# Every other tile of a streaming GELU-and-multiply kernel in two steps, of seven rows and of one

## Chip, cores, metric

One Trainium2 chip, one core of it. The metric is the device time of one execution in microseconds (us). Differences are told as the ratio of the means of the runs of the same rounds, with a 95% interval; within 2% counts as the same.

## The reference

The input is 32 x 512 x 2048 floats (134 MB), the output 32 x 512 x 1024 (67 MB).

```python
def reference(x):
    half_dim = x.shape[-1] // 2
    x1, x2 = x[..., :half_dim], x[..., half_dim:]
    gelu_x1 = 0.5 * x1 * (1 + erf(x1 / np.sqrt(2)))
    return (gelu_x1 * x2).astype(np.float32)
```

## The kernel before

The 16384 rows are cut into 16 tiles of 128 partitions x 8 rows. A tile is loaded whole (8.39 MB) through the Scalar engine's DMA queue, GELU runs in place on the Scalar engine (ACT), the multiply on the Vector engine (DVE), and the result (4.19 MB) is stored through the Sync engine's queue. There are two input and two output buffers. Tiles 0 and 15 are done in steps of 2, 2 and 4 rows, so that the start and the end are short. A transfer is issued when an engine hands it to its queue, and has landed when whatever waits for it may go on; in the profile a q behind an engine's name marks that issuing side.

```python
x_tiles = [xpool.tile([P, R, dim], x.dtype, name=f"x{k}_tile") for k in range(2)]
o_tiles = [opool.tile([P, R, half], out.dtype, name=f"o{k}_tile") for k in range(2)]
...
load(0)
load(1)
for i in range(n_tiles):
    x_tile, o_tile = x_tiles[i % 2], o_tiles[i % 2]
    last = i == n_tiles - 1
    pieces = i == 0 or last
    steps = ((0, 2), (2, 4), (4, 8)) if pieces else ((0, 8),)
    for lo, hi in steps:
        rows = slice(lo, hi)
        gelu = ... nc.scalar.activation(out=x_tile[:, rows, :half], in_=x_tile[:, rows, :half], func=GELU)
        mul = nc.vector.tensor_mul(out=o_tile[:, rows, :], in0=x_tile[:, rows, :half], in1=x_tile[:, rows, half:])
        ...
        if pieces and hi % 4 == 0:
            part = slice(hi - 4, hi)
            nc.sync.dma_start(out=o_t[i][:, part, :], in_=o_tile[:, part, :])
    if not pieces:
        nc.sync.dma_start(out=o_t[i], in_=o_tile)
    ...
    if i + 2 < n_tiles:
        load(i + 2)        # into the buffer that tile i has just left
```

Of the kernel before, what the change touches and what calls it, by code (L numbers as in the profile page):

```python
# [1 line left out]

# [4 lines left out]

GELU = mybir.ActivationFunctionType.Gelu


@with_exitstack
def kernel(
    ctx: ExitStack,
    tc: tile.TileContext,
    x: bass.AP,
    out: bass.AP,
):











    nc = tc.nc
    P = nc.NUM_PARTITIONS  # L30

    x_flat = x.flatten_outer_dims()
    out_flat = out.flatten_outer_dims()
    n_rows, dim = x_flat.shape
    half = dim // 2

    R = 8
    x_t = x_flat.rearrange("(n p r) d -> n p r d", p=P, r=R)
    o_t = out_flat.rearrange("(n p r) d -> n p r d", p=P, r=R)
    n_tiles = x_t.shape[0]  # L40

    xpool = ctx.enter_context(tc.tile_pool(name="xpool", bufs=1))
    opool = ctx.enter_context(tc.tile_pool(name="opool", bufs=1))
    x_tiles = [xpool.tile([P, R, dim], x.dtype, name=f"x{k}_tile") for k in range(2)]
    o_tiles = [opool.tile([P, R, half], out.dtype, name=f"o{k}_tile") for k in range(2)]

    def no_wait(ins, others):
        for other in others:
            tc.declare_no_dep(ins, other, reason="implied by another wait")

    x_users, o_users = ([], []), ([], [])
    loads = {}

    def load(i):
        x_tile = x_tiles[i % 2]
        loads[i] = []
        for rows in (slice(0, 4), slice(4, 8)) if i == 0 else (slice(0, 8),):
            dma = nc.scalar.dma_start(out=x_tile[:, rows, :], in_=x_t[i][:, rows, :])  # L58
            loads[i].append(dma.ins)
# [4 lines that stand above are left out]
        x_tile, o_tile = x_tiles[i % 2], o_tiles[i % 2]  # L64
        last = i == n_tiles - 1
        pieces = i == 0 or last
        steps = ((0, 2), (2, 4), (4, 8)) if pieces else ((0, 8),)
        gelus, muls = [], []
        for lo, hi in steps:
            rows = slice(lo, hi)  # L70
            gelu = tc.keep_in_program_order(
                nc.scalar.activation(  # L72
                    out=x_tile[:, rows, :half], in_=x_tile[:, rows, :half], func=GELU
                )
            )
            no_wait(gelu.ins, x_users[i % 2])
            mul = nc.vector.tensor_mul(  # L77
                out=o_tile[:, rows, :],
                in0=x_tile[:, rows, :half],
                in1=x_tile[:, rows, half:],  # L80
            )
            no_wait(mul.ins, loads[i] + x_users[i % 2] + o_users[i % 2])
            gelus.append(gelu.ins)
            muls.append(mul.ins)
# [5 lines that stand above are left out]
        x_users[i % 2].extend(gelus + muls + loads[i])  # L90
        o_users[i % 2].extend(muls)
        if i + 2 < n_tiles:
            load(i + 2)


# [1 line left out]
_INS = ['x']  # L97
_OUTS = [((32, 512, 1024), 'float32')]


# [23 lines left out]
```

## Time and profile before

| | before |
|---|---|
| time, median of 3 runs | 470.62 us |
| span of the profiled run | 468.8 us |
| busy: DVE, ACT | 30%, 24% |
| moved, over the span | 201.33 MB at 429 GB/s |
| one tile period in the steady part | 29.0 us |
| a load, from issue to landing | 42.2 us (median) |

The lines of the profile are in the prediction.

### The profile page before, as it was taken

How to read it: one execution, taken by the hardware profiler on the slowest of the kernel's cores; microseconds unless marked ns; L12 is line 12 of the kernel's file. 1: busy time of each engine (PE TensorE's matmuls, PEld its weight loads, DVE VectorE, ACT ScalarE, POOL GpSimd, SP SyncE). 2: the span in 40 equal slices, each digit the busy share in tenths (PEclk: the TensorE clock that was granted, in tenths of full speed). 3: DMA queues.
4: the chain of work that ended last, by engine and by line, in shares of the span. 5: the costliest groups of instructions: out<-in, count | busy, mean ns of one | idle time of the engine just before them, and what ended most of it. 6: DMA issues, size and time to landing. Idle time of an engine off the chain costs nothing.

```text
span 468.8 us, 150 instructions
## 1 busy us (share of the span) xinstructions
DVE 139.5 (30%) x20; ACT 114.2 (24%) x21; POOL 0.2 (0%) x4
## 2 busy tenths in 40 slices
DVE  0330333407033070430704207052070510606142
ACT  1320505041050410505005050140501405023060
POOL 0000000000000000000000000000000000000000
DMA  8999999999999999999999999999999999999998
GB/s 358 447 447 447 414 389 495 403 403 447 481 414 403 447 403 492 403 433 417 492 403 403 447 492 403 403 447 447 447 403 439 411 492 403 403 447 492 403 403 358
DMA packets 5041, 201.33 MB, mean 429 GB/s; under 512 B 561, under 2 KB 561, under 8 KB 561
## 3 DMA queue, kind: packets, MB, share of 16 engines
q10 hardware_dynamic: 2448, 134.22, 66.3%
q1 hardware_dynamic: 2592, 67.11, 33.2%
q14 instruction: 1, 0.00, 0.0%
HBM read 134.22 MB, written 67.11 MB: 429 GB/s over the span
## 4 chain that ended last, share of the span: by engine, by line
DMA 72%; DVE 14%; ACT 12%; ACTq 1%; issue 0%
DMA x_tile<-in_x_dram 72%; DVE o_tile L77 14%; ACT x_tile L72 12%; ACTq L119 0%; ACTq L58 0%
## 5 line engine op out<-in xcount | busy, mean ns | idle before, releaser
L77 DVE TENSOR_TENSOR o_tile<-x_tile 128x8192 f32<-128x8192 f32 (+2 forms) x20 | 139.5, 6985 | 320.7 <-ACT x_tile L72 320.7
L72 ACT ACTIVATE x_tile<-x_tile 128x8192 f32<-128x8192 f32 (+2 forms) x20 | 113.0, 5662 | 339.4 <-DMA x_tile<-in_x_dram 339.4
L72 ACT ACT_TABLE_LOAD x1 | 1.3, 1283 | 2.1 <-issue 2.1
L108 POOL MEMSET const-bfloat16-1.0<- 128x1 bf16 x1 | 0.1, 102 | 0.0
L108 POOL MEMSET const-uint8-127<- 128x1 uint8 x1 | 0.1, 102 | 0.0
L108 POOL MEMSET const-float32-0.0<- 128x1 f32 x1 | 0.1, 99 | 0.2 <-issue 0.2
L108 POOL MEMSET const-float32-1.0<- 128x1 f32 x1 | 0.1, 99 | 0.0
## 6 DMA issues: line engine op xcount, KB each, us to landing
out_dram<-o_tile SPq DMA_DIRECT2D x14, 4096.0 KB, 42.4
x_tile<-in_x_dram ACTq DMA_DIRECT2D x2, 4096.0 KB, 16.8
out_dram<-o_tile SPq DMA_DIRECT2D x4, 2048.0 KB, 18.0
x_tile<-in_x_dram ACTq DMA_DIRECT2D x15, 42.2
```

The lines of the kernel that those rows point to most:

```text
L72: nc.scalar.activation(out=x_tile[:, rows, :half], in_=x_tile[:, rows, :half], func=GELU)
L77: mul = nc.vector.tensor_mul(out=o_tile[:, rows, :], in0=x_tile[:, rows, :half], in1=x_tile[:, rows, half:],)
L108: nc = _bacc.Bacc("TRN2", target_bir_lowering=False, num_devices=1)
```

## The change

The intent: let the multiply of an odd tile start once seven eighths of its GELU are done. Its end, and with it the next load into that buffer, then comes earlier by about one row's GELU, less what the added instructions cost.

```diff
-        steps = ((0, 2), (2, 4), (4, 8)) if pieces else ((0, 8),)
+        steps = ((0, 2), (2, 4), (4, 8)) if pieces else ((0, 7), (7, 8)) if i % 2 else ((0, 8),)
```

## The prediction

> **What bounds the kernel now.** I read the page first, for what is full. Engines, then the transfer lines of the slices, then the queues:
>
> ```profile
> span 468.8 us, 150 instructions
> DVE 139.5 (30%) x20; ACT 114.2 (24%) x21; POOL 0.2 (0%) x4
> DMA  8999999999999999999999999999999999999998
> q10 hardware_dynamic: 2448, 134.22, 66.3%
> q1 hardware_dynamic: 2592, 67.11, 33.2%
> DMA x_tile<-in_x_dram 72%; DVE o_tile L77 14%; ACT x_tile L72 12%; ACTq L119 0%; ACTq L58 0%
> ```
>
> The two compute engines are under a third busy. The 16 DMA engines are at "9" in every slice but the first and the last, and the two queues' packet times add up to 66.3 + 33.2 = 99.5% of 16 engines' span. That leaves next to no idle transfer time to win. The last line, however, puts 14 + 12 = 26% of the chain that ended last on the multiply and the GELU. The chain names whatever released the next step, not whatever was full, so I had to look at whether these 26% are really in series with the transfers.
>
> The busy view by stretches, one tile period (29 us) each, decides it. Columns: stretch and length, busy time of DVE, ACT, POOL with instruction counts, clock, DMA share, GB/s.
>
> ```profile
> 71.00:100.00 29.00, 8.69 (x1) 7.03 (x1) 0.00 (x0) 1.00 1.00 434
> 100.00:129.00 29.00, 8.69 (x1) 7.03 (x1) 0.00 (x0) 1.00 1.00 434
> 158.00:187.00 29.00, 8.69 (x1) 7.03 (x1) 0.00 (x0) 1.00 1.00 434
> ```
>
> Share 1.00 and 434 GB/s, period after period, while a GELU and a multiply run in each. No period has a hole while compute runs.
>
> Why compute makes no hole shows in the timeline (start, length, engine, instruction, idle before it):
>
> ```profile
> 158.41 7.03 ACT L72 ACTIVATE x_tile<-x_tile 128x8192 f32<-128x8192 f32 x1 [22.00 <-DMA x_tile<-in_x_dram]
> 165.47 8.69 DVE L77 TENSOR_TENSOR o_tile<-x_tile 128x8192 f32<-128x8192 f32 x1 [20.33 <-ACT x_tile L72]
> 174.20 0.37 ACTq L58 DMA_DIRECT2D x_tile<-in_x_dram  x1
> 187.40 7.03 ACT L72 ACTIVATE x_tile<-x_tile 128x8192 f32<-128x8192 f32 x1 [21.96 <-DMA x_tile<-in_x_dram]
> ```
>
> Tile 5 landed at 158.4; its buffer is free when its multiply ends at 174.2, and only then is the load of tile 7 issued into it. But tile 6 is still on its way until 187.4. The load of tile 7 therefore lies queued for 187.4 - 174.2 = 13.2 us and moves from 187.4 to 216.4, when its own GELU starts: 29.0 us. The chain of waits books all of 174.20 to 216.37 as transfer:
>
> ```profile
> 158.41 7.04 ACT x_tile L72
> 165.47 8.70 DVE o_tile L77
> 174.20 42.17 DMA x_tile<-in_x_dram
> 216.39 7.04 ACT x_tile L72
> ```
>
> 42.17 = 13.2 queued + 29.0 moving. So the path through compute has 13.2 us of slack per tile, and the 26% of the chain lie beside the other tile's transfer.
>
> **What the Trainium skill says.** "DMA: Bandwidth & Descriptors", section "Queues, rings and completion order": each DMA engine round-robins between the queue rows that it has work for, a packet at a time. The trace agrees: an 8.39 MB load at 434 GB/s would take 19.3 us by itself, but takes 29.0, just the time of 8.39 + 4.19 MB, so one load and one store share each period. Same page, "Where 436 GB/s comes from": the ports' ceiling is 435.2 GB/s; the trace has 434 in every steady period, so I take the transfers to be at their ceiling. "VectorE: DVE Perf Modes", section "The TRN2 errata": an fp32 tensor_tensor takes (N+151)/0.96 ns, for N = 8192 that is 8691; the trace has 8693. "ScalarE: Activation LUTs", "What ACT_TABLE_LOAD costs": an ACTIVATE takes 186 ns + 0.833 N, 7010 for 8192; the trace has 7029. So splitting costs a fixed 0.15 to 0.2 us per added instruction.
>
> **The change part by part.** Tiles 1, 3, 5, 7, 9, 11 and 13 (tiles 0 and 15 keep their own steps) get a GELU on rows 0-6 and one on row 7, and likewise two multiplies. The instruction order shows seven more instructions on each of the two engines, no other reordering; loads and stores stay whole and as many, the store still follows the last multiply, the next load still waits for it. The first multiply of an odd tile takes over the wait for the store that frees its output buffer.
>
> Durations by shape, before:
>
> ```profile
> L77 DVE TENSOR_TENSOR o_tile<-x_tile 128x8192 f32<-128x8192 f32 x14 | 121.7, 8693 | 283.0 <-ACT x_tile L72 283.0
> L72 ACT ACTIVATE x_tile<-x_tile 128x8192 f32<-128x8192 f32 x14 | 98.4, 7029 | 302.0 <-DMA x_tile<-in_x_dram 302.0
> L77 DVE TENSOR_TENSOR o_tile<-x_tile 128x2048 f32<-128x2048 f32 x4 | 9.0, 2289 | 30.0 <-ACT x_tile L72 30.0
> L72 ACT ACTIVATE x_tile<-x_tile 128x2048 f32<-128x2048 f32 x4 | 7.4, 1901 | 31.5 <-DMA x_tile<-in_x_dram 31.5
> ```
>
> GELU slope: (7029 - 1901)/6144 = 0.8346 ns per element; so 7168 takes 7029 - 1024 x 0.8346 = 6174 ns and 1024 takes 1901 - 855 = 1046. Multiply slope: (8693 - 2289)/6144 = 1.0423; 7168 takes 7626, 1024 takes 1222.
>
> Removed per odd tile: 7.03 + 8.69. Added: 6.17 + 1.05 on ACT (7.22, 0.19 more), 7.63 + 1.22 on DVE (8.85, 0.16 more). Over seven tiles 1.3 us of ACT and 1.1 us of DVE, all in engines that idle some 20 us a tile.
>
> Moved: from landing of an odd tile to the issue of the next load into its buffer it is now 7.04 + 0.02 + 8.70 + 0.02 = 15.78 us. Afterwards 6.18 + 0.02 + 7.63 + 0.02 + 1.22 + 0.02 = 15.09; row 7's GELU (1.05) runs beside the 7.63 of the first multiply. So the issue comes 0.69 us earlier on seven tiles. What that is worth: the load goes into a queue that is occupied for another 13.2 us, so it waits 13.9 instead and lands when it did. The store goes 0.69 us earlier into its queue too; its time from issue to landing has a median of 42.4 us, more than the period of 29.0, so that queue also has an earlier store to finish first.
>
> The end: the last load lands when all before it have moved, as before, and tile 15 is unchanged.
>
> ```profile
> 448.55 7.22 ACT L72 ACTIVATE x_tile<-x_tile 128x2048 f32<-128x2048 f32 x3 [21.98 <-DMA x_tile<-in_x_dram]
> 455.02 5.57 SPq L87 DMA_DIRECT2D out_dram<-o_tile  x2
> 455.80 4.42 DVE L77 TENSOR_TENSOR o_tile<-x_tile 128x4096 f32<-128x4096 f32 x1 [0.81 <-ACT x_tile L72]
> ```
>
> From 448.5 to the end, about 8.4 MB of stores remain (tile 14's and tile 15's 4.19 MB each); at 434 GB/s that is 19.3 us, to 467.8, of a span of 468.8. So the tail is also filled by transfers, and these bytes don't change. The sum on the path is 0.0 us: 470.6 stays 470.6.
>
> **The rivals.** First: the chain is literally right and every saved 0.69 us of an odd tile counts, 7 x 0.69 = 4.8 us: 465.8. For it speaks only that the chain does run through the odd tiles, 1, 3, 5 and so on; against it the 13.2 us of queueing and the 434 GB/s. Even then it is 1.0%, inside the 2%.
> Second: the output-buffer wait takes over. An odd tile's first multiply starts 0.86 us earlier (7.03 - 6.17), and the store of two tiles before must have landed. That store is issued at a multiply's end and lands 42.4 us later; the next multiply in the buffer starts 58.0 - 8.7 = 49.3 us after that end. Slack 6.9 us, some 6.0 with the change: no wait, 470.6. Were the slack wrongly read, the multiply would start when it does now, and would still hurt nothing within the 13.2 us.
> Third: the shifted issues, or GELU running beside the multiply on the same tile, disturb the engines or the transfers. Were the multiply slowed by a fifth, 1.7 us, it would still fit in 13.2. Only a change of the transfers' own rate would show: 1% of it is 4.7 us, so 475.3. Against it: same packets, same sizes, same two queues, and in tile 0 and tile 15 GELU and multiply already overlap with multiplies of 2285 to 2289 ns.
>
> **Range and chances.** The three runs of before lie within 0.34 us. I add a few tenths for the way the last packets of the two queues fall: 470.6, range 470.1 to 471.2. Faster by 2% would need 9.4 us, twice what the first rival can give: 0.005. Slower by 2% needs an effect on the transfer rate that I see no cause for: 0.01.
>
> **What would show it right or wrong.** Right: steady periods still 29.0 us at 434 GB/s; odd tiles' time from issue to landing 0.7 us longer (42.2 to 42.9), even tiles' unchanged; new groups near 6174, 1046, 7626 and 1222 ns; last load landing near 448.5. Wrong: an odd load's issue-to-landing that stays at 42.2 with a shorter period, so that the first rival's microseconds appear; or a DMA share below 1.00, or a multiply released by a store, in a steady period.

## The result, and the profile after

The changed kernel takes 470.54 us (median of 6 runs, 470.34 to 473.33), the kernel before 470.66 (6 runs). The ratio is 1.0007 with an interval of 0.9984 to 1.003: the same. A ratio is the mean time of one kernel's fast runs over that of the other's of the same rounds, so it isn't quite the ratio of the medians quoted here; the one run at 473.33 is what lifts it over 1.

The page of the changed kernel, its span, its busy times and the DMA line of the slices:

```profile
span 468.6 us, 164 instructions
DVE 140.0 (30%) x27; ACT 114.9 (25%) x28; POOL 0.2 (0%) x4
DMA  8999989999999999999999999999999999999998
```

Fourteen more instructions, 0.5 us more work on DVE and 0.7 on ACT, and a DMA line that is as full as before. The steady periods, by stretches (the same columns as in the prediction), an odd tile and an even one:

```profile
100.00:129.00 29.00, 8.76 (x2) 7.12 (x2) 0.00 (x0) 1.00 1.00 434
129.00:158.00 29.00, 8.69 (x1) 7.03 (x1) 0.00 (x0) 1.00 1.00 434
```

DMA share 1.00 and 434 GB/s in both. Now the chain that ended last, at the same tile as shown of before:

```profile
158.25 6.18 ACT x_tile L72
164.45 8.77 DVE o_tile L77 x2
173.25 42.98 DMA x_tile<-in_x_dram
216.25 6.18 ACT x_tile L72
```

Compute did become shorter: 158.25 to 173.25 is 15.00 us, where it was 158.41 to 174.20, 15.79. The load that follows takes just that much longer from issue to landing, 42.98 instead of 42.17. From one GELU of the buffer to the next there are 58.00 us here and 57.98 before. The load of an even tile, from the timeline, its issue and the GELU that waited for it:

```profile
145.04 0.37 ACTq L58 DMA_DIRECT2D x_tile<-in_x_dram  x1
187.25 7.03 ACT L72 ACTIVATE x_tile<-x_tile 128x8192 f32<-128x8192 f32 x1 [21.89 <-DMA x_tile<-in_x_dram]
```

42.2 us, unchanged. The groups by shape show what the pieces cost (busy us, mean ns):

```profile
L77 DVE TENSOR_TENSOR o_tile<-x_tile 128x7168 f32<-128x7168 f32 x7 | 53.4, 7625 | 139.5 <-ACT x_tile L72 139.5
L72 ACT ACTIVATE x_tile<-x_tile 128x7168 f32<-128x7168 f32 x7 | 43.2, 6176 | 152.8 <-DMA x_tile<-in_x_dram 152.8
...
L77 DVE TENSOR_TENSOR o_tile<-x_tile 128x1024 f32<-128x1024 f32 x7 | 8.5, 1219 | 0.0
...
L72 ACT ACTIVATE x_tile<-x_tile 128x1024 f32<-128x1024 f32 x7 | 7.3, 1040 | 0.0
```

So far the traces agree with one reading: time taken from compute goes into the queue. They don't prove it. That a larger saving, or a larger delay, goes the same way, and how far, had to be tried. The theory: the transfers are always full, and compute has a slack that swallows the gain. The main rival: compute and load of one buffer are in series as the chain shows them, and the gain was lost to something else, such as the added instructions or the overlap of the two engines. All runs of other kernels below gave right results unless said otherwise, and all were timed beside the kernel before on the same chip.

### The profile page after: what moved, and what is told of

Same layout as the page of the kernel before. It is cut to its first block, busy times and chain, and to the rows that moved or that the text cites. A ratio compares the mean times of both kernels' runs of the same rounds, so it can differ in the third digit from the quotient of the medians.

```text
span 468.6 us, 164 instructions
## 1 busy us (share of the span) xinstructions
DVE 140.0 (30%) x27; ACT 114.9 (25%) x28; POOL 0.2 (0%) x4
## 4 chain that ended last, share of the span: by engine, by line
DMA 73%; DVE 14%; ACT 10%; ACTq 1%; issue 0%
DMA x_tile<-in_x_dram 73%; DVE o_tile L77 14%; ACT x_tile L72 10%; ACTq L119 0%; ACTq L58 0%
## 5 line engine op out<-in xcount | busy, mean ns | idle before, releaser
L77 DVE TENSOR_TENSOR o_tile<-x_tile 128x7168 f32<-128x7168 f32 (+4 forms) x27 | 140.0, 5213 | 320.0 <-ACT x_tile L72 320.0
L72 ACT ACTIVATE x_tile<-x_tile 128x7168 f32<-128x7168 f32 (+4 forms) x27 | 113.6, 4242 | 338.6 <-DMA x_tile<-in_x_dram 338.6
## 6 DMA issues: line engine op xcount, KB each, us to landing
x_tile<-in_x_dram ACTq DMA_DIRECT2D x15, 42.2
```

## Experiments

**The changed kernel once more**, unedited, because of the run at 473.33.

> The changed kernel once more, in more rounds, because one of its six runs took 473.33 us. Theory (transfers full, compute has 13.2 us of slack a tile): median 470.3 to 470.9, ratio 0.999 to 1.001; 473 is rare and not of this kernel's making. Rival (the split brings a second, slower state with it): again one run or more near 473 in five, none for the kernel before.

470.42 us (5 runs, 470.40 to 470.79), ratio 0.9998 (0.9984 to 1.0011). One of eleven runs of this kernel was near 473, and none of the kernel before was. The trace is not of that run, so its cause stays open.

**A larger saving: all tiles in pieces.**

```diff
-        steps = ((0, 2), (2, 4), (4, 8)) if pieces else ((0, 8),)
+        steps = ((0, 2), (2, 4), (4, 8))
```

> Every tile in steps of two, two and four rows, the steps that tile 0 and tile 15 have: multiply ends about 1.9 + 2.3 + 2.3 + 4.4 = 10.9 us after landing instead of 15.8, so the next load is issued 4.9 us earlier, seven times the change's 0.69. Theory: 470.6, at most 2.4 us to either side. Rival (chain in series): 7 x 4.9 = 34 us less, 436.

470.93 us, ratio 1.0006 (0.9993 to 1.002). The multiply ended 11.7 us after landing, not 10.9: the last one waits for all of GELU's three pieces (7.2 us) before its own 4.4. So 4.1 us were saved a tile, not 4.9, and issue to landing rose by 4.1, from 42.2 to 46.3 us. Five times the change's saving is still worth nothing.

**A larger saving yet: nearly no GELU** in tiles 1 to 14 (wrong result).

```diff
-                    out=x_tile[:, rows, :half], in_=x_tile[:, rows, :half], func=GELU
+                    out=x_tile[:, rows, :cols], in_=x_tile[:, rows, :cols], func=GELU   # cols = half if pieces else 8
```

> GELU of tiles 1 to 14 on 8 of 1024 columns only, wrong result on purpose: some 6.8 us less on the path of each tile, ten times what the change takes away. Theory: 470.6, at most 2.4 us (one load packet) to either side from the order of packets; odd and even loads' issue to landing rises from 42.2 to about 49 us. Rival (chain in series): seven odd tiles, 7 x 6.8 = 48 us less, 423.

471.19 us, ratio 1.0013 (0.9999 to 1.0027). From its chain:

```profile
158.39 0.27 ACT x_tile L73
...
167.40 49.09 DMA x_tile<-in_x_dram
```

The GELU has shrunk from 7.04 to 0.27 us, and the load takes 49.09 instead of 42.2. The rival would have had 423. The chain's ACT share is thus not time that can be won.

**A delay: odd tiles multiply twice**, which changes no result.

```diff
+            if not pieces and i % 2:
+                for _ in range(1):
+                    again = nc.vector.tensor_mul(out=o_tile[:, rows, :], in0=..., in1=...)   # as the multiply above it
```

> Odd tiles 1 to 13 multiply twice: 8.7 us more on the path from landing to the next load's issue, within the slack of 13.2 us. Theory: 470.6, within 0.5; issue to landing of the odd loads falls from 42.2 to 33.5 us, periods stay 29.0. Rival (the chain is literally in series): 7 x 8.7 = 61 us more, 531.

474.57 us (two runs at 473.8, two near 475.4), ratio 1.0085 (1.0069 to 1.0101). This was not within 0.5 of 470.6, so the expectation missed, though the rival's 531 is far off. The profiled run took 473.8; those near 475.4 have no trace. In the steady periods it was met: issue to landing 33.4 us, periods 29.00 us at 434 GB/s. In the trace the loss sits at the first odd tile. Its timeline and, below, the stretch with the hole:

```profile
62.99 8.69 DVE L85 TENSOR_TENSOR o_tile<-x_tile 128x8192 f32<-128x8192 f32 x1
71.72 0.33 SPq L98 DMA_DIRECT2D out_dram<-o_tile  x1
71.78 0.34 ACTq L58 DMA_DIRECT2D x_tile<-in_x_dram  x1
```

```profile
69.00:72.00 3.00, 2.69 (x1) 0.00 (x0) 0.00 (x0) 1.00 0.21 87
```

The load of tile 3 is issued at 71.78, when tile 2's has already landed (71.4 in the kernel before); the queue is empty, and the DMA share of that stretch is 0.21. (A stretch counts a packet where it starts, so a short one is rough; by the packet records the 16 engines were idle from 71.0 to 72.6.) At tile 1 the slack is smaller than later, because the first loads share the engines with fewer stores and land closer together: 71.4 - 63.0 = 8.4 us in the kernel before, against 13.2 in the steady part.

**A delay beyond the slack: three times.**

```diff
-                for _ in range(1):
+                for _ in range(2):
```

> Odd tiles 1 to 13 multiply three times: 17.4 us more, 4.2 us over the slack. Theory: now it costs, at least 7 x 4.2 = 29 us if every microsecond over the slack is lost once, and up to about 50 us if the stores that come late leave holes as well: 495 to 525, with a DMA share below 1.00 in the steady periods. Rival (chain in series): 7 x 17.4 = 122 us more, 592. Rival (slack is much more than 13.2 us): 471.

526.78 us, ratio 1.1193 (1.1178 to 1.1208): more than expected of a slack of 13.2. The reason is in the chain. A load issued into an empty queue took 32.0 us to land, not the 29.0 of a load that follows another. So the slack that a delay may use is 58.0 - 15.8 - 32.0 = 10.2 us in the steady part, and 8.4 - 3.0 = 5.4 at tile 1. With these, six tiles lose 17.45 - 10.2 = 7.25 us each (the trace: 65.3 us from GELU to GELU of the buffer instead of 58.0) and tile 1 loses 12.0: 55.5 in sum; measured 56.2. This was worked out after the run, so it was put to three more.

**Twice, in tile 1 alone** (the condition becomes `if i == 1`).

> Multiply twice in tile 1 alone. Theory: 8.7 - 5.4 = 3.3 us are lost once, near the start: 473.8 to 474.6, as with all seven doubled. Rival (each doubled tile costs a little): 471.2.

473.67 us, ratio 1.0065 (1.0049 to 1.0082). One delayed tile near the start costs 3.1 us, which the theory put at 3.3; the time is 0.1 under the range expected.

**Twice and three rows more, in tiles 3 to 13.**

```diff
-            if not pieces and i % 2:
-                for _ in range(1):
+            if not pieces and i % 2 and i > 1:
+                for again_rows in (rows, slice(0, 3)):
```

> Odd tiles 3 to 13 multiply twice and rows 0 to 2 a third time, 8.7 + 3.3 = 12.0 us more: under the 13.2 us of the prediction, over the 10.2 us that the tripled run points to. Theory (10.2): six tiles lose 1.8 us each, 11 us: 479 to 484. Rival (13.2 as predicted): 470.6.

482.16 us, ratio 1.0245 (1.023 to 1.026): 11.6 us lost where 10.2 us of slack say 11 and 13.2 say none. Its chain shows the load behind the added multiplies:

```profile
188.22 32.05 DMA x_tile<-in_x_dram
```

By the packet records the load ahead had its last packets end at 188.4 to 188.8, so the queue was all but empty when this one was issued, and its own first packet began at 190.96, 2.7 us after the issue.

**Six rows twice, in tiles 3 to 13** (`for again_rows in (slice(0, 6),)`).

> Odd tiles 3 to 13 multiply rows 0 to 5 a second time, 6.6 us more, so that a load is still issued some 6.6 us before the one ahead of it ends (4.1 us in the run that doubled all eight rows and fell to 473 to 482[...]). Theory (it costs only where the load comes later than those 4 us): 470.6 within 0.5, issue to landing of odd loads 35.6 us, periods 29.0. Rival (any second multiply in the steady periods costs in proportion): 6.6 / 8.7 of 11 us, 479.

Time from issue to first packet: in the empty queue it was 2.7 us (71.78 to 74.50 in the run with all seven doubled).

470.60 us (5 runs), ratio 0.9999 (0.9986 to 1.0013).

```profile
174.34 6.57 DVE o_tile L85
...
180.98 35.55 DMA x_tile<-in_x_dram
```

6.57 us more compute, and issue to landing is down to 35.55 from 42.2, 6.6 less. Seen from the other side it is the same exchange as in the change.

**All eight rows twice, in tiles 3 to 13**: between the last two.

> Multiply twice in odd tiles 3 to 13 but not in tile 1. The last runs say: a load issued into an empty queue takes 32.0 us to land, so the steady slack is 58.0 - 15.8 - 32.0 = 10.2 us, and at tile 1 it is 71.4 - 63.0 - 3.0 = 5.4. Theory (the 4 us of the run with all seven came from tile 1 alone): 8.7 fits in 10.2, 470.6 within 0.5. Rival (each doubled tile costs a little): 6/7 of 3.9 us, 474.

Inconclusive. Its four runs took 473.25, 481.59, 481.72 and 482.09 us; the clock was 1.00 in all, but three are over 1.5% above the fastest, so they count as slow and there is no ratio. Even the fastest is 2.7 us over the kernel before, so 8.7 us did not simply fit. A delay of 6.6 us is free and one of 12.0 costs 11.6; near the edge, at 8.7, the time jumps from run to run. The packet records of the profiled run (481.72 us) show where its time went. When the load of tile 4 ended at 128.5, 3.7 us after tile 5's was issued, ten engines began at once with a packet of tile 5's load, but six took a packet of the store first and began the load at 129.8 or later. From there the engines drifted apart: their shares of one load ended 0.3 us apart at tile 4 and 3.3 us apart at tile 15. A load has landed when the last engine is done, so the next issue came later each time: the last one came only 0.7 us before the load ahead of it ended on the first engine. In the run with all seven doubled each engine took a store's packet first, so the load was needed only 4.7 us after its issue, and the engines stayed within 0.5 us. That this is why the times jump fits, but is not shown: only one of these runs has a trace, and what decides which runs fall into it stays open.

**No slack: one input buffer.** The kernel before and the changed one with a single input buffer. Now no load can be queued behind another, and compute is in series for certain.

```diff
-... name=f"x{k}_tile") for k in range(2)]
+... name=f"x{k}_tile") for k in range(1)]
-    load(0)
-    load(1)
+    load(0)
-        if i + 2 < n_tiles:
-            load(i + 2)
+        if i + 1 < n_tiles:
+            load(i + 1)
```

> The kernel before with one input buffer instead of two, so that no load is queued behind another and the slack is gone. Theory: a tile takes 29.0 us of transfer, 15.8 of compute and some 2.5 from issue to first packet and from last packet to GELU, 47 us: about 740 us, with a DMA share near 0.6. It is the base for the next run.

749.43 us (749.20 to 749.88), 9 us over the rough 740: a tile takes 48.0 us (201.63 to 249.67), of which 32.2 go from a load's issue to its landing. The DMA share of a period is 0.64.

> The same one-buffer kernel with this case's change put into it. Theory: without the slack each odd tile gives its 0.69 us, 7 x 0.69 = 4.8 us less than the one-buffer kernel before the change. Rival (the split is worth nothing even in series, because of its added instructions or a slower overlap): the same time, within 1 us.

744.15 us (743.54 to 744.39). The means are 749.49 and 744.01, a ratio of 0.993 (no interval for this pair, but their runs don't overlap): 5.5 us less, a little over the 4.8 expected. The timelines, one tile each: the GELU's start and the next load's issue, without the split,

```profile
249.67 7.03 ACT L71 ACTIVATE x_tile<-x_tile 128x8192 f32<-128x8192 f32 x1 [41.01 <-DMA x_tile<-in_x_dram]
...
265.45 0.37 ACTq L58 DMA_DIRECT2D x_tile<-in_x_dram  x1
```

and with it:

```profile
248.22 7.12 ACT L71 ACTIVATE x_tile<-x_tile 128x7168 f32<-128x7168 f32 x2 [40.88 <-DMA x_tile<-in_x_dram]
...
263.23 0.37 ACTq L58 DMA_DIRECT2D x_tile<-in_x_dram  x1
```

15.78 and 15.01 us: 0.77 us a tile, 7 x 0.77 = 5.4. The split is worth what it saves where nothing is queued. This rules out that its own costs ate the gain.

**The end: the last tile whole** (`pieces = i == 0`).

> The kernel before with its last tile in one step and one store. Nothing is queued behind the last load, so here compute is on the path. Theory: last load lands at 448.5, 15.8 of compute, then some 12.4 us for 4.19 MB from issue to landing (7.7 us is 2.1 MB's): 476.7 of span, 478.5 in time, 8 us slower. Rival (the tail hides compute as the middle does): 470.6.

478.07 us, ratio 1.0158 (1.0145 to 1.0172). The last store's issue, and the stretch around it:

```profile
464.32 0.33 SPq L89 DMA_DIRECT2D out_dram<-o_tile  x1
```

```profile
458.00:468.00 10.00, 6.30 (x1) 0.00 (x0) 0.00 (x0) 1.00 0.37 157
```

After the last load there is nothing to hide compute behind, and the DMA share falls to 0.37; by the packet records the engines were idle from 457.6 to 465.2, 7.6 us, and the run is 7.4 us longer. Steps pay here, and the kernel already has them.

No version beat both kernels. The packet records of the kernel before have its first load packet 1.7 us into the span and its last store packet end at 467.6 of 468.8. Between 3 and 467 us its 16 DMA engines were idle for 0.13 us on average. In that stretch there is nothing for a change of compute to win.

## Why the prediction was right

The time (470.54 against 470.6, range 470.1 to 471.2) and the verdict were right, and so were the steps that carry them. One of the six runs, at 473.33, lay outside the range, and why is open.

- **The transfers are the bound.** 434 GB/s and share 1.00 in each steady period after the change, and no gain from savings up to 6.8 us a tile (nearly no GELU). The load and the store take turns on each engine, as the prediction had it: in the steady part a load packet of 65,536 bytes (2.42 us) and a store packet of 32,768 (1.21 us) alternate.
- **The issue comes earlier, and the load waits longer.** Predicted 0.69 us and 42.9 us from issue to landing; measured 0.79 and 42.98. The last load landed at 448.3, with 448.5 predicted. The piece durations were within 6 ns of the estimates (6176 for 6174, 1040 for 1046, 7625 for 7626, 1219 for 1222). What the sum missed is that the two multiplies overlap: 7625 + 1219 = 8844 ns, but the pair took 8.77 us, where the prediction had 7.63 + 0.02 + 1.22 = 8.87. "Perfetto Trace Analysis", section "Optimizing Scalar/DVE Operations", has it: the write-acknowledgement half of an instruction's overhead overlaps with the next instruction. The trace agrees that they overlap, by some 0.08 us, though not what it is that overlaps. For the same reason the prediction's 0.15 to 0.2 us per added instruction were too much: the profile's page shows 0.5 us for seven on DVE and 0.7 on ACT, 0.07 and 0.10 each.
- **The first rival falls** with the one-buffer pair: the gain it counts is real (5.3 us by the medians) but only where no load waits in the queue.
- **The second and third rivals fall.** No multiply was released by a store in the changed trace, and neither the transfer rate nor the durations under overlap moved.

One size was wrong, though it decided nothing here: the slack of "13.2 us per tile". That is how long a load lies behind the one before it, but a load that comes into an empty queue needs 3.0 us more from issue to landing. A delay may use 10.2 us at most by that working, and 5.4 at the first odd tile, where the prediction used the steady number for all seven; measured, 6.6 us were free in tiles 3 to 13 and 8.7 were not. By the same working the prediction's third rival, a multiply slowed by 1.7 us, would still have fitted.

## What to carry to other kernels

Before shortening a step on the chain, compare the time from issue to landing with the time that a load issued into an empty queue takes (here 42.2 and 32.0 us, with a store sharing the engines in both); what is over is queueing, and a saving ahead of it only lengthens the queueing. Doubling the step (a delay that changes no result) tests for a slack of that length: here it cost 3.9 us, where a step in series would have cost 61. And taking the buffers down to one shows whether the saving is real. A slack read from the steady part holds neither for the first tiles nor for the last, so look at those by themselves.

## What the Trainium skill lacked or had wrong

- "DMA: Bandwidth & Descriptors", "Latency and other measured facts", gives about 600 ns to the first byte of a DMA from the sync and scalar queues. By the packet records, which show when a packet begins and not its first byte, the first load here was issued at 0.74 us and had its first packet at 1.75, 1.0 us later. A load issued at 71.78, 0.06 us after a store, with nothing in either queue, had its first at 74.50, 2.7 us later, after a packet of the store on each engine (72.55 to 74.5; odd tiles multiplied twice). The page has no figure for two issues close together.
- The same page, "Where 436 GB/s comes from", says that for HBM to SBUF transfers the HBM side, about 358 GB/s, binds. The sentence lacks its condition, which the page gives elsewhere: about 358 is each core's when both cores on one HBM domain stream. With one core running, this kernel moved 434 GB/s of loads from and stores to HBM in every steady period, next to the page's ceiling of 435.2.
- No page that I read says that the 16 engines' shares of a load can drift apart when it is issued just ahead of the end of the one before (by 3.7 us here; ends 0.3 us apart grew to 3.3), or that a kernel's time can then jump between runs (473.25 to 482.09 us, at the full clock).
